# One pass of a hybrid decoder step rewritten as a pipeline in program order, sample group's linear attention moved to the third pass, PSUM banks divided anew

## The chip, the cores and the metric

The kernel runs on one core of a Trainium2 chip. The metric is device time in microseconds (us), measured over several executions; a profiled execution gives the trace. Before: 3477.97 us, median of 3 runs (3465.1 to 3479.64).

## The reference

One inference step of a two-layer decoder over a prompt of 4096 tokens and a sample group of 32 tokens (8 sequences of 4), model width 1024, in fp32:

```python
def even_layer(x, s5_state0, gla_state0, p):              # layer 0
    proj = rms_norm(x, p['norm_g']) @ p['w_in']
    u, gate_a, q, k, v, a_low, gate_b = split(proj)       # 512,512,256,256,512,16,512
    y, s5_last = s5_scan(u, s5_state0, ...)               # 32 groups, 64 complex states
    z = gelu(y)
    z = z * sigmoid(z @ p['w_glu'] + p['b_glu'])
    out_a = z * silu(gate_a)
    log_a = log_sigmoid(a_low @ p['w_gate'] + p['b_gate']) / 16
    o, gla_last = gla_chunked(q / 8, k, v, log_a, gla_state0)   # 4 heads, 64 x 128 states
    out_b = rms_norm(o, p['gla_norm_g']) * silu(gate_b)
    return x + concat([out_a, out_b]) @ p['w_out'], s5_last, gla_last
# layer 1: windowed grouped-query attention (window 128, 16 heads, sink logits), output projection
```

Outputs are both groups' activations and all new states.

## The kernel before

Every fp32 product on TensorE is made of three fp16 products: x and the weights are split into a high and a low part (xh, xl; wh, wl), scaled by powers of two, and `mmB` (L327, L328, L329) or `mmA` (L336, L337, L338) runs xh·wh, xl·wh, xh·wl into one PSUM bank, an `mm` tile. A power of two needs a bound on the weights, so each weight block is loaded twice: once for the bound (`bound_all`, loads at L221, squares by row at L192 on ScalarE and L195 on VectorE) and once to be split (`load_w`, L240 and L241).

The prompt is worked in 16 windows of 256 tokens, in passes:

- **Pass A** (`phaseA`, L683): per window, load x (L254, four tiles of 256 KB, 12 buffers), square it (ScalarE L756), add the squares (VectorE L760, L763, L764), sum over channels with a tiny matmul (L766), take the power -1/2 on GpSimd (L287), broadcast it (`rbcast`, L297 and L300), multiply and split x (`xsplit`: x times rb L311 on VectorE, xh L312 on ScalarE, xl L313 on GpSimd), then the projection to u, 96 matmuls with weights wuh and wul. u is evicted at L813 and stored to DRAM (u_d, L822) by ScalarE. `stage` holds all up to the statistics and returns `split`. Tables for the scan (`tables`, lines around L500 to L590) and the weights of pass B (`loads`) are made beside it.
- **Pass B** (`phaseB`, L866): per window a second load of x, projections to gate b, q, k, v (`instream`), the chunked linear attention (`core`, L1031 on; `head_norm` L1003, `og_split` L1019 to L1025, results stored as ob), pieces of the scan of the S5 branch (`s5_units`; U is loaded from u_d at L626), and `bounds` for the weights still to come. In windows 14 and 15 (SMP0, SMP1) the sample group's linear attention is added (`sample`, L1093): its projections (L351, folded at L367), then 8 states of 128 KB, each loaded, updated by L1232 and L1234 and stored.
- **Pass C** (`phaseC`, L1314): gate a, the half-GLU, the output projection, the rest of the sample group's first layer in windows 0 to 3.
- **Phase 2** (L1540 on): the second layer.

`merge` (L44) interleaves Python generators by their given costs; a scheduler then orders the instructions of each engine by priority in a simulated time of its own. `high_priority(HP)` around `stage` and `split` lets them move ahead of all else. Each DMA stands in the queue of the engine that issues it and keeps that queue's order: most are SyncE's (SP).

PSUM has 8 banks. Before, pass A uses four for `mm` tiles (pm0, pm1, pmx0, pmx1), three for small tiles `pt` (pta, ptb, ptc) and one for the scan (p0v); pass B two for `mm`, three for `pt`, one for the scan, two for the attention (pat); pass C three and two. `Rota` takes the banks of its list in turn:

```python
pms = self.pms = Rota(self.pta, self.ptb, self.ptc)     # pass A
pmm = Rota(*pm, *(self.pool(f"pmx{i}", es=ea, space=PSUM) for i in range(2)))
pmm, pms = Rota(*self.pm), Rota(self.pta, self.ptb, self.ptc)            # pass B
merge((ustream(), 170.0), (tables(), 18.0), (loads(), 66.0))             # end of pass A
merge((core(w), 14.0), (instream(w + 1), 46.0), (self.some(s, SB), SB), side)   # window of B
```

Of the kernel before, what the change touches and what calls it, by code (L numbers as in the profile page):

```python
# [9 lines left out]
F32 = mybir.dt.float32  # L10
F16 = mybir.dt.float16
# [9 lines left out]
SEQ = 4096  # L21
# [11 lines left out]
SB, SB1, BG, SC = 8.0, 14.0, 13.0, 14.0  # L33
SMP0, SMP1 = 14, 15
# [54 lines left out]
class K:  # L89
# [592 lines left out]
    def phaseA(self):  # L682
# [25 lines left out]
        pm = [self.pool(f"pm{i}", space=PSUM) for i in range(2)]  # L708
# [14 lines left out]
        wp = self.pool("w0", bufs=2, es=ea, side="right")  # L723
# [26 lines left out]
        def stage(n, blk0, xs):  # L750

            ps = pms.tile([128, 512], F32, name="pt")
            m = min(n, 128)
# [10 lines left out]
            nc.vector.tensor_add(sq[:, 0], sq[:, 0], sq[:, 1])  # L764
            for i in range((n + 127) // 128):
                nc.tensor.matmul(ps[0:m, i:i + 1], sq[:, 0, 128 * i:128 * i + m], self.onesf[:, 0:1],  # L766
                                 start=(i == 0), stop=True, skip_group_check=True)
            self.rms(ps, n, self.rst0, blk0, wp, self.rs0)

            def split():  # L770
                rb = self.rbcast(self.rst0, blk0, n, wp, pms, tag="pt")
                return self.xsplit(xs, n, rb, hp)

            return split

        xsm = stage(NS, 32, xsm)()
        xw = [x0] + [self.xload(xp, I["xT"], 256 * i, 256) for i in (1,)]
        x0 = stage(256, 0, x0)()
        xw.append(self.xload(xp, I["xT"], 512, 256))
# [3 lines left out]
        def ustream():  # L783

            x, nextx = xsm, x0
            split = stage(256, 2, xw[1])
            us = wp.tile([128, 4, 4, 8], F32, name="uss", bufs=1)
            ps = pmm.tile([128, 2, 256], F32, name="mm")
            for ct in range(4):
                self.mmB(ps[:, 0, NS * ct:NS * ct + NS], wuh, wul, 0, 128 * ct, *x)  # L790
# [69 lines left out]

    def phaseB(self):
# [11 lines left out]
        pmm, pms = Rota(*self.pm), Rota(self.pta, self.ptb, self.ptc)  # L875
# [4 lines left out]
        self.sog_d = self.dr.tile([128, 2, 4, NS], F16, name="sog_d")  # L880
# [15 lines left out]
        sr2 = self.scaled(ri, 2.0**-11, "sr2")  # L896
        sr8 = self.scaled(ri, 2.0**-13, "sr8")
# [105 lines left out]
        def head_norm(po, gb, m):  # L1003

            Q = Pc if m > NS else self.smp
            ss = Q.tile([128, 4], F32, name="ss", bufs=2)
            og = Q.tile([128, 512], F32, name="og", bufs=2) if m > NS else Q.tile([128, 512], F32, name="p")
            for h in range(4):
                nc.scalar.activation(og[0:m, 128 * h:128 * h + 128], po[h], AF.Square, bias=0.0, scale=1.0,
                                     accum_out=ss[0:m, h:h + 1])  # L1010
            nc.vector.tensor_scalar(ss[0:m], ss[0:m], 1.0 / 128, EPS, op0=OP.mult, op1=OP.add)  # L1011
            rs = Q.tile([128, 4], F32, name="rs", bufs=2)
            nc.gpsimd.tensor_tensor(rs[0:m], ss[0:m], self.mhalf[0:m, 0:4], op=OP.pow)  # L1013
            nc.vector.tensor_scalar(rs[0:m], rs[0:m], 2.0**-20, None, op0=OP.mult)
            for h in range(4):
                s = slice(128 * h, 128 * h + 128)
                nc.vector.scalar_tensor_tensor(og[0:m, s], po[h], rs[0:m, h:h + 1], gb[0:m, s], op0=OP.mult, op1=OP.mult)
            return og

        def og_split(og, m, oh, ol, t):  # L1020
            pt = pms.tile([128, 4, 128], F32, name="pt")[:, :, 0:m]
            for h in range(4):
                nc.tensor.transpose(pt[:, h], og[0:m, 128 * h:128 * h + 128], self.identf[0:m, 0:m])
            nc.scalar.activation(oh[:, :, t], pt, AF.Copy, bias=0.0, scale=1.0)
            nc.vector.tensor_sub(ol[:, :, t], pt, oh[:, :, t])  # L1025

        def core(w):
            W = Ws[w]
            yield 2.0
            for b in range(2):  # L1030
# [46 lines left out]
                og = head_norm([pa[0][:, 2], pa[1][:, 2], pa[0][:, 3], pa[1][:, 3]], W["gb"][b], 128)  # L1077
# [1148 lines left out]
```

## Time and profile before

| | us |
|---|---|
| median of 3 runs | 3477.97 (3465.1 to 3479.64) |
| the profiled execution's own time | 3474.53 |
| its span, first to last instruction | 3472.7 |
| PE (TensorE matmul) busy | 3178.1 (92%) |
| VectorE (DVE) busy | 2038.0 (59%) |
| ScalarE (ACT) busy | 1688.3 (49%) |
| GpSimd (POOL) busy | 1305.8 (38%) |
| mean granted TensorE clock | 0.951 |
| pass A | 0 to 352 |
| pass B, from its first to its last projection | 371 to 1317 |
| pass C, from its first matmul | 1377 |
| phase 2 | 1965 to 3472 |

A busy time counts an instruction's whole duration, so PE is also "busy" where its clock is halved. A wait names the instruction that stood still, the one it waited for, and the time lost. SPq is the queue of DMAs that SyncE issues; "L626 <- DMA ud<-us" there means that a load at L626 stood until a store of us to ud had landed, and all behind it in the queue stood too.

### The profile page before, as it was taken

To read this page: it belongs to the slowest core of one execution; us is meant where nothing else is said; L and a number is where in the kernel's file an instruction comes from. 1 tells how busy PE (TensorE), PEld (TensorE's weight loads), DVE (VectorE), ACT (ScalarE), POOL (GpSimd) and SP (SyncE) were. 2 spreads that over 40 slices of the span, in tenths; PEclk is the share of its full clock that TensorE was granted. 3 is DMA by queue.
4 is the path that set the end of the run, shared out by engine and by line. 5 is a ranking of instruction groups with operands and counts; after the bars stand their busy time and mean duration, and the time that the engine had idled before them with its cause. 6 is when DMAs were issued, how large, how long until landed. Compare 5 with 4: busy or idle time off the path is not lost.

```text
span 3472.7 us, 69409 instructions
## 1 busy us (share of the span) xinstructions
PE 3178.1 (92%) x27160; PEld 2472.0 (71%) x27160; DVE 2038.0 (59%) x4837; ACT 1688.3 (49%) x4044; POOL 1305.8 (38%) x1459
## 2 busy tenths in 40 slices
PE   4667798888989897999999999999999999999999
PEld 3556576666767665788888866777777777777777
DVE  6743576766567644543333357666666666666666
ACT  5444455445454642432222236655555555555565
POOL 4623322323232210122122265555555545555552
PEclk9878898999999996999999999999999999999999
DMA  7554644322232414544344322111111111111111
GB/s 190 106 114 86 183 132 118 88 61 78 59 78 68 133 51 123 176 124 110 104 120 118 87 48 64 38 37 36 36 42 40 40 40 40 40 40 40 40 30 41
DMA packets 359370, 277.72 MB, mean 80 GB/s; under 512 B 157985, under 2 KB 313585, under 8 KB 358897
## 3 DMA queue, kind: packets, MB, share of 16 engines
q1 hardware_dynamic: 316032, 231.28, 24.9%
q10 hardware_dynamic: 38912, 33.58, 3.7%
q0 software_dynamic: 4096, 8.43, 0.7%
q8 instruction: 213, 3.49, 0.4%
q14 instruction: 117, 0.95, 0.1%
HBM read 194.49 MB, written 78.50 MB: 79 GB/s over the span
## 4 chain that ended last, share of the span: by engine, by line
PE 64%; DMA 11%; DVE 10%; ACT 6%; issue 5%; POOL 3%; SPq 1%; ACTq 0%; DVEq 0%; POOLq 0%
PE mm L327 11%; PE mm L328 11%; PE mm L329 11%; PE mm L336 6%; PE mm L338 6%; PE mm L337 6%; DMA wst<-in_w_in 4%; PE po L1845 3%; DMA x<-in_xT 2%; PE pt L1803 2%; PE ps L1784 1%; PE ps L1785 1%; DVE z L638 1%; POOL xl L313 1%; PE pt L1653 1%
## 5 line engine op out<-in xcount | busy, mean ns | idle before, releaser
L313 POOL TENSOR_TENSOR xl<-x,xh 128x512 f16<-128x512 f32 (+1 forms) x196 | 236.0, 1223 | 359.6 <-ACT xh L312 351.4
L1768 ACT ACTIVATE Sc<-Sc,ng,rq 128x128 f32<-128x128 f32 x512 | 245.9, 482 | 138.7 <-DVE ng L1762 138.4
L327 PE MATMUL mm<-ogh,woh 128*128 128x256 f16 x960 | 261.7, 273 | 1.8 <-DVE xr L1889 1.8
L328 PE MATMUL mm<-ogl,woh 128*128 128x256 f16 x960 | 261.7, 273 | 0.7 <-POOL ogl L1857 0.7
L329 PE MATMUL mm<-ogh,wol 128*128 128x256 f16 x960 | 261.7, 273 | 0.0
L1796 POOL TENSOR_TENSOR Pl<-Sc,Ph 128x512 f16<-128x512 f32 x128 | 153.0, 1196 | 283.6 <-ACT Ph L1795 223.1
L337 PEld LDWEIGHTS <-xh 128*128 128x128 f16 x1536 | 155.8, 101 | 130.1 <-issue 43.9
L336 PEld LDWEIGHTS <-xh 128*128 128x128 f16 x1536 | 156.2, 102 | 119.9 <-ACT xh L312 16.3
L338 PEld LDWEIGHTS <-xl 128*128 128x128 f16 x1536 | 156.1, 102 | 115.0 <-issue 6.9
L328 PEld LDWEIGHTS <-woh 128*128 128x128 f16 x2112 | 206.8, 98 | 38.9 <-issue 15.5
L327 PEld LDWEIGHTS <-woh 128*128 128x128 f16 x2112 | 207.2, 98 | 27.1 <-issue 3.7
L329 PEld LDWEIGHTS <-wol 128*128 128x128 f16 x2112 | 206.9, 98 | 24.4 <-issue 1.8
L336 PE MATMUL mm<-wi1gbh,xh 128*128 128x264 f16 x512 | 155.9, 305 | 50.3 <-DVE k L995 18.9
L268 POOL TENSOR_TENSOR acc<-acc,sq 128x512 f32<-128x512 f32 x48 | 61.9, 1289 | 367.6 <-ACT sq L267 367.6
L1013 POOL TENSOR_TENSOR rs<-ss,mhalf 128x4 f32<-128x4 f32 (+1 forms) x33 | 36.8, 1114 | 372.7 <-DVE ss L1011 326.7
L327 PE MATMUL mm<-xh,wuh 128*128 128x256 f16 (+1 forms) x544 | 154.0, 290 | 19.7 <-ACT xh L312 19.3
L328 PE MATMUL mm<-xl,wuh 128*128 128x256 f16 (+1 forms) x544 | 154.4, 290 | 9.1 <-POOL xl L313 9.1
L338 PE MATMUL mm<-wi1gbh,xl 128*128 128x264 f16 x512 | 153.6, 303 | 3.6 <-POOL xl L313 3.6
L337 PE MATMUL mm<-wi1gbl,xh 128*128 128x264 f16 x512 | 155.4, 305 | 0.0
L329 PE MATMUL mm<-xh,wul 128*128 128x256 f16 (+1 forms) x544 | 154.2, 289 | 0.0
L327 PE MATMUL mm<-oh,woh 128*128 128x256 f16 x512 | 140.2, 274 | 10.9 <-DVE xr L1419 9.6
L1805 ACT ACTIVATE PT<-pt 128x1024 f16<-128x1024 f16 x128 | 129.3, 1011 | 39.9 <-PE pt L1803 39.9
(728 smaller groups left out, 10980.7 us busy)
## 6 DMA issues: line engine op xcount, KB each, us to landing
wst<-in_w_in SPq DMA_DIRECT2D x132, 256.0 KB
x<-in_xT SPq DMA_DIRECT2D x128, 256.0 KB
xr<-in_xT SPq DMA_DIRECT2D x64, 256.0 KB
h_d<-xr SPq DMA_DIRECT2D x64, 256.0 KB
x<-h_d SPq DMA_DIRECT2D x64, 256.0 KB
xr<-h_d SPq DMA_DIRECT2D x64, 256.0 KB
out_yT<-xr SPq DMA_DIRECT2D x64, 256.0 KB
wst<-in_w_out SPq DMA_DIRECT2D x48, 256.0 KB
```

Of the source, the lines that this page charges most:

```text
L313: nc.gpsimd.tensor_sub(l, x, h)
L327: nc.tensor.matmul(ps, wh[:, k0 + k, c], xh[k], start=(k == 0), stop=False)
L328: nc.tensor.matmul(ps, wh[:, k0 + k, c], xl[k], start=False, stop=False)
L329: nc.tensor.matmul(ps, wl[:, k0 + k, c], xh[k], start=False, stop=(k == n - 1))
L336: nc.tensor.matmul(ps, xh[k][:, t], wh[:, k, c0:c1], start=(k == 0), stop=False)
L337: nc.tensor.matmul(ps, xh[k][:, t], wl[:, k, c0:c1], start=False, stop=False)
L338: nc.tensor.matmul(ps, xl[k][:, t], wh[:, k, c0:c1], start=False, stop=(k == n - 1))
L1768: nc.scalar.activation(Sc[:, i], Sc[:, i], AF.Exp, bias=ng[:, i:i + 1], scale=scale[:, i:i + 1], accum_out=de[:, i:i + 1])
L1796: nc.gpsimd.tensor_sub(Pl, Sc, Ph)
L1803: nc.tensor.transpose(pt[:, a, i], s[:, i], self.ident16)
L1805: nc.scalar.activation(PT, pt.rearrange("p a i n -> p (a i) n"), AF.Copy, bias=0.0, scale=1.0)
L1845: nc.tensor.matmul(po[c].rearrange("p i n -> p (i n)"), vx[:, c], pend2[kv][1][p2][:, 4 * lo:4 * lo + 4].rearrange("p i n -> p (i n)"), st ...
```

## The change

1. **Pass of u.** `stage` and its closure become `squares`, `statistics` and `split`; `high_priority` goes. Windows 0 and 1 are made ready ahead of the loop. In window i, `split` of window i+1 and the load of window i+3 stand at the start, `squares` of i+2 after the first quarter of the projection, `statistics` of i+2 after the first half. The pool `w0` (sq, us, rb) moves to the left side of SBUF.
2. **PSUM.** Three `pm` banks for projections in all passes; the small banks are two (ptc goes); pass A has one further `mm` bank.
3. **Sample group.** In pass B, windows 8 and 9 now do its four projections, and store them unfolded to DRAM (sp_d). The folds, gates and 8 state updates (`sample_gla`) run in pass C, where the sample takes windows 0 to 9 with cost 3.4 each, not 0 to 3 with 4.0. `bounds` therefore has windows 0 to 7 to run in. `head_norm` and `og_split` become methods.

```diff
-SB, SB1, BG, SC = 8.0, 14.0, 13.0, 14.0
-SMP0, SMP1 = 14, 15
+SB, SB1, BG, SC = 8.0, 14.0, 13.0, 7.0
+SMP0, SMP1, SMP2 = 8, 9, 10
...
-        pm = [self.pool(f"pm{i}", space=PSUM) for i in range(2)]
+        pm = [self.pool(f"pm{i}", space=PSUM) for i in range(3)]
...
-        self.ptc = self.pool("ptc", es=self.eps, space=PSUM)
-        pms = self.pms = Rota(self.pta, self.ptb, self.ptc)
+        pms = self.pms = Rota(self.pta, self.ptb)
...
-        pmm = Rota(*pm, *(self.pool(f"pmx{i}", es=ea, space=PSUM) for i in range(2)))
+        pmm = Rota(*pm, self.pool("pmx", es=ea, space=PSUM))
...
-        wp = self.pool("w0", bufs=2, es=ea, side="right")
+        wp = self.pool("w0", bufs=2, es=ea)
...
-                    x = nextx
-                    i = 4 * w + h + 1
-                    if i < 16:
-                        with self.tc.high_priority(HP):
-                            nextx = split()
-                            if i + 2 < 16:
-                                xw.append(self.xload(xp, I["xT"], 256 * (i + 2), 256))
+                    i = 4 * w + h
+                    if 1 <= i < 15:
+                        x.append(split(256, 2 * (i + 1), xw[i + 1]))
+                        if i + 3 < 16:
+                            xw.append(load(i + 3))
...
-                            self.mmB(ps[:, k], wuh, wul, 0, 256 * c + 128 * k, *x)
+                            self.mmB(ps[:, k], wuh, wul, 0, 256 * c + 128 * k, *x[i])
+                            if c + k == 0 and i + 2 < 16:
+                                sq = squares(256, xw[i + 2])
...
-                        if c == 0 and i + 1 < 16:
-                            with self.tc.high_priority(HP):
-                                split = stage(256, 2 * (i + 1), xw[i + 1])
+                        if c == 0 and i + 2 < 16:
+                            statistics(256, 2 * (i + 2), sq)
...
-        pmm, pms = Rota(*self.pm), Rota(self.pta, self.ptb, self.ptc)
+        pmm, pms = Rota(*self.pm), Rota(self.pta, self.ptb)
...
+            for b, c0, c1 in (("gb", 0, 512), ("gb", 512, 528), ("qk", 0, 512), ("v", 0, 512)):
+                p = self.keep(Q.tile([128, 512], F32, name="p"), self.parts(*W1[b], 0, c0, c1, x, pmm))
+                nc.sync.dma_start(self.sp_d[b, c0][:, 0:c1 - c0], p)
+                yield 3.0
...
-                  (self.some(smp, 4.0) if w < 4 else None, 4.0))
+                  (self.some(smp, 3.4) if w < SMP2 else None, 3.4))
```

The order of SP's DMAs in the middle of pass A, before. Rows with "x4" stand for several in a row; x is a load of pass A's next windows, U a load for the scan from what ScalarE stored as ud, wst weights.

```order
56 L626 DMA U<-ud_0_119 16x4x64 x3
57 L254 DMA x<-in_xT 128x2x256 x6
58 L626 DMA U<-ud_0_119 16x4x64
59 L254 DMA x<-in_xT 128x2x256
60 L626 DMA U<-ud_0_119 16x4x64 x2
61 L254 DMA x<-in_xT 128x2x256
62 L626 DMA U<-ud_0_119 16x4x64 x5
63 L254 DMA x<-in_xT 128x2x256 x8
64 L626 DMA U<-ud_0_123 16x4x64 x6
65 L254 DMA x<-in_xT 128x2x256
66 L626 DMA U<-ud_0_123 16x4x64 x2
67 L254 DMA x<-in_xT 128x2x256 x3
```

In the changed kernel no U is loaded within pass A; the first is at its row 105. Its order at the end of pass A: rows 89 to 93 end with the last loads of x of pass A, row 101 is the first of pass B. Of rows 94 to 100, one load is the last of load_w and 39 are the bounds' (in_w_in, in_w_glu and in_w_out are the weights in DRAM).

```order
89 L254 DMA x<-in_xT 128x2x256 x2
90 L221 DMA wst<-in_w_in 128x512
91 L254 DMA x<-in_xT 128x2x256
92 L221 DMA wst<-in_w_in 128x512
93 L254 DMA x<-in_xT 128x2x256
94 L221 DMA wst<-in_w_in 128x512 x9
95 L221 DMA wst<-in_w_glu 128x512 x4
96 L221 DMA wst<-in_w_out 128x512 x13
97 L912 DMA wga<-in_w_gate 16x256
98 L914 DMA bga<-in_b_gate 128x2
99 L221 DMA wst<-in_w_out 128x512 x3
100 L221 DMA wst<-in_w_in 128x512 x11
```

Before, pass B's first x (row 122 of that order) stands ahead of all of the bounds' loads; now 39 of them stand ahead of it.

PE at the end of pass B, before: L1240, L1232 and the L1023 with a 128x32 output are the sample group's, the others belong to the core of windows 14 and 15; pass C's first matmul comes four rows behind the last one shown.

```order
11950 L1240 MATMUL pt<-identf,z 32x128 x4
11951 L1232 MATMUL pt<-v,p 64x128 x8
11952 L1051 MATMUL pt<-identf,kt 128x128 x4
11953 L1023 MATMUL pt<-identf,p 128x32 x4
11954 L1023 MATMUL pt<-identf,og 128x128 x4
11955 L1072 MATMUL pt<-v,kT 64x128 x4
11956 L1023 MATMUL pt<-identf,og 128x128 x4
11957 L1072 MATMUL pt<-v,kT 64x128 x4
11958 L1066 MATMUL pa_14472<-Sm,q_14077 128x128
11959 L1066 MATMUL pa_14473<-Sm,q_14077 128x128
11960 L1066 MATMUL pa_14472<-Sm,q_14172 128x128
11961 L1066 MATMUL pa_14473<-Sm,q_14172 128x128
```

The same place in the changed kernel (L885 is og_split, L1041, L1065, L1070, L1076 the core).

```order
11911 L1076 MATMUL pt<-v,kT 64x128 x4
11912 L885 MATMUL pt<-identf,og 128x128 x2
11913 L1041 MATMUL pa_14231<-q_14009,k_14010 128x128
11914 L1041 MATMUL pa_14231<-q_14101,k_14102 128x128
11915 L885 MATMUL pt<-identf,og 128x128
11916 L1041 MATMUL pa_14232<-q_14009,k_14010 128x128
11917 L1041 MATMUL pa_14232<-q_14101,k_14102 128x128
11918 L885 MATMUL pt<-identf,og 128x128
11919 L1065 MATMUL pa_14231<-v,attm_3536 128x128 x2
11920 L1070 MATMUL pa_14231<-Sm,q_14009 128x128
11921 L1070 MATMUL pa_14231<-Sm,q_14101 128x128
11922 L1065 MATMUL pa_14232<-v,attm_3537 128x128 x2
```

None of the sample group's rows is left here; four rows further on pass C's first matmul follows, and og_split's last transposes come behind it.

## Rows read from the trace of the kernel before

**Rows 1.** Page, part 1: each engine's busy time, share of the span, instructions

```profile
PE 3178.1 (92%) x27160; PEld 2472.0 (71%) x27160; DVE 2038.0 (59%) x4837; ACT 1688.3 (49%) x4044; POOL 1305.8 (38%) x1459
```

**Rows 2.** Windows: span, us; busy us (instructions) per engine; clock; DMA share, GB/s

```profile
150.00:200.00 50.00, 29.41 (x212) 23.29 (x212) 26.02 (x37) 19.98 (x34) 20.54 (x20) 0.74 0.50 86
200.00:250.00 50.00, 38.20 (x303) 32.16 (x301) 25.73 (x45) 24.90 (x40) 16.35 (x16) 0.83 0.60 122
250.00:300.00 50.00, 40.53 (x297) 32.66 (x298) 22.20 (x45) 23.50 (x44) 15.44 (x15) 0.80 0.67 122
300.00:325.00 25.00, 14.70 (x116) 12.21 (x114) 17.29 (x21) 12.20 (x19) 12.29 (x10) 0.80 0.36 89
325.00:350.00 25.00, 25.00 (x232) 22.42 (x230) 0.00 (x0) 8.15 (x9) 5.14 (x7) 1.00 0.16 57
350.00:375.00 25.00, 8.90 (x58) 7.13 (x56) 14.29 (x21) 8.61 (x16) 11.79 (x11) 0.64 0.69 193
375.00:700.00 325.00, 286.86 (x2038) 214.38 (x2036) 220.93 (x605) 168.10 (x428) 96.22 (x102) 0.91 0.43 124
700.00:1150.00 450.00, 408.49 (x2993) 308.30 (x2991) 296.69 (x786) 219.97 (x538) 114.77 (x122) 0.93 0.26 67
...
1250.00:1325.00 75.00, 71.21 (x595) 51.66 (x592) 30.64 (x126) 34.81 (x107) 11.71 (x13) 0.96 0.11 36
1325.00:1375.00 50.00, 31.81 (x158) 19.81 (x158) 17.54 (x62) 6.08 (x28) 3.57 (x4) 0.50 0.43 135
1375.00:1400.00 25.00, 23.87 (x205) 18.91 (x203) 15.53 (x38) 14.01 (x29) 0.67 (x1) 0.95 0.83 239
1400.00:1965.00 565.00, 549.72 (x5016) 487.18 (x5016) 224.50 (x348) 169.75 (x272) 122.05 (x117) 0.99 0.43 118
```

**Rows 3.** Waits of SP's DMA queue, 50 to 365 us: total us, times, longest

```profile
SPq L626 <- DMA ud<-us: 48.4, 7, 13.9
SPq L254 <- POOL xl L313: 44.8, 22, 7.9
...
SPq L254 <- DMA ud<-us: 19.2, 2, 14.4
```

**Rows 4.** Groups by line, 100 to 350 us: busy us, mean ns, idle before and releasers

```profile
L327 PE MATMUL mm<-xh,wuh 128*128 128x256 f16 x435 | 127.1, 293 | 2.4 <-ACT xh L312 2.4
...
L756 ACT ACTIVATE sq<-x 128x512 f32<-128x512 f32 x43 | 26.6, 626 | 77.6 <-DMA x<-in_xT 64.2 <-DMA ud<-us 12.4 <-DVE sq L760 0.6
...
L766 PE MATMUL pt<-onesf,sq 128*128 128x1 f32 x48 | 9.2, 296 | 54.2 <-DVE sq L764 24.1 <-ACT Ks L544 20.9 <-DVE X L589 9.2
```

**Rows 5.** Waits of PE, 365 to 1215 us: total us, times, longest

```profile
PE mm L336 <- DVE k L995: 18.9, 6, 4.9
PE pt L1023 <- DVE og L1017: 16.2, 5, 7.6
PE mm L336 <- DVE gb L946: 12.3, 4, 5.6
```

**Rows 6.** Chain that ended last, 1310 to 1380 us: start, duration, engine, work

```profile
1335.96 2.19 DMA out_gla_s<-S
1338.16 2.46 DMA S<-in_gla
1340.75 0.36 DVE S L1234
...
1359.72 0.61 ACT ogh L1024
1360.35 0.69 DVE ogl L1025
1361.07 5.73 DMA ob<-ogl
...
1368.49 8.95 DMA xl<-xp
```

**Rows 7.** PE groups by line, 1150 to 1375 us: busy us, mean ns, idle before

```profile
L1232 PE MATMUL pt<-v,p 32*64 32x128 f32 x64 | 10.8, 432 | 9.7 <-DVE S L1234 5.9 <-DVE p L1227 3.8
```

More of the change, by code (lines that the diff above doesn't have):

```diff
@@ L764, in stage, with statistics, split, ready @@
             nc.vector.tensor_add(sq[:, 0], sq[:, 0], sq[:, 1])
+            return sq[:, 0]
+        def statistics(n, blk0, sq):
+            ps = pms.tile([128, 512], F32, name="pt")
+            m = min(n, 128)
             for i in range((n + 127) // 128):
-                nc.tensor.matmul(ps[0:m, i:i + 1], sq[:, 0, 128 * i:128 * i + m], self.onesf[:, 0:1],
+                nc.tensor.matmul(ps[0:m, i:i + 1], sq[:, 128 * i:128 * i + m], self.onesf[:, 0:1],
                                  start=(i == 0), stop=True, skip_group_check=True)
             self.rms(ps, n, self.rst0, blk0, wp, self.rs0)
[L770 to L779, printed above, removed]
+        def split(n, blk0, xs):
+            return self.xsplit(xs, n, self.rbcast(self.rst0, blk0, n, wp, pms, tag="pt"), hp)
+        def ready(n, blk0, xs):
+            statistics(n, blk0, squares(n, xs))
+            return split(n, blk0, xs)
+        load = lambda i: self.xload(xp, I["xT"], 256 * i, 256)
+        xsm = ready(NS, 32, xsm)
+        xw = [x0, load(1)]
+        x = [ready(256, 0, x0)]
+        xw.append(load(2))
+        x.append(ready(256, 2, xw[1]))
+        xw.append(load(3))
         nc.sync.dma_start(self.g1, I["g1"])
@@ L859, in rbload, with head_norm, og_split @@
         return rb
+    def head_norm(self, Q, po, gb, m):
+        nc = self.nc
+        ss = Q.tile([128, 4], F32, name="ss", bufs=2)
+        og = Q.tile([128, 512], F32, name="og", bufs=2) if m > NS else Q.tile([128, 512], F32, name="p")
+        for h in range(4):
+            nc.scalar.activation(og[0:m, 128 * h:128 * h + 128], po[h], AF.Square, bias=0.0, scale=1.0,
+                                 accum_out=ss[0:m, h:h + 1])
+        nc.vector.tensor_scalar(ss[0:m], ss[0:m], 1.0 / 128, EPS, op0=OP.mult, op1=OP.add)
+        rs = Q.tile([128, 4], F32, name="rs", bufs=2)
+        nc.gpsimd.tensor_tensor(rs[0:m], ss[0:m], self.mhalf[0:m, 0:4], op=OP.pow)
+        nc.vector.tensor_scalar(rs[0:m], rs[0:m], 2.0**-20, None, op0=OP.mult)
+        for h in range(4):
+            s = slice(128 * h, 128 * h + 128)
+            nc.vector.scalar_tensor_tensor(og[0:m, s], po[h], rs[0:m, h:h + 1], gb[0:m, s], op0=OP.mult, op1=OP.mult)
+        return og
+    def og_split(self, pms, og, m, oh, ol, t):
+        nc = self.nc
+        pt = pms.tile([128, 4, 128], F32, name="pt")[:, :, 0:m]
+        for h in range(4):
+            nc.tensor.transpose(pt[:, h], og[0:m, 128 * h:128 * h + 128], self.identf[0:m, 0:m])
+        nc.scalar.activation(oh[:, :, t], pt, AF.Copy, bias=0.0, scale=1.0)
+        nc.vector.tensor_sub(ol[:, :, t], pt, oh[:, :, t])
     def phaseB(self):
@@ L1001, in instream @@
                 prep(w + 1)
[L1003 to L1025, printed above, removed]
         def core(w):
@@ L1087, in finish @@
                 tiles[:] = [P.tile([128, 4, NW], F16, name=f"og{x}") for x in "hl"]
-            og_split(og, 128, *tiles, slice(128 * b, 128 * b + 128))
+            self.og_split(pms, og, 128, *tiles, slice(128 * b, 128 * b + 128))
             if b == 1:
@@ L1144, in sample @@
-            lm = Q.tile([128, 4, n], F32, name="z")
-            l, bb = lm[:, 0:2], lm[:, 2:4]
-            pg = pmi.tile([128, 512], F32, name="pt")
-            for j in range(2):
-                g = pg[:, n * j:n * j + n]
-                nc.tensor.matmul(g, wga[:, 128 * j:128 * j + 128], alT, start=True, stop=True)
-                nc.scalar.activation(l[:, j], g, AF.Abs, bias=bga[:, j:j + 1], scale=1.0)
-                nc.vector.tensor_scalar(bb[:, j], g, bga[:, j:j + 1], 0.0, op0=OP.add, op1=OP.min)
@@ L1152, in sample @@
-            nc.scalar.activation(l, l, AF.Exp, bias=0.0, scale=-1.0)
-            nc.scalar.activation(l, l, AF.Ln, bias=1.0, scale=1.0)
-            for j in range(2):
-                for c in range(0, n, 4):
-                    t = slice(c, c + 4)
-                    nc.vector.tensor_tensor_scan(bb[:, j, t], bb[:, j, t], l[:, j, t], 0.0, op0=OP.add, op1=OP.subtract)
-            yield 0.5
-            p = proj("qk")
-            yield 1.5
-            qz = Q.tile([128, 2, 2, n], F32, name="q")
@@ L1440, in sample @@
         def sample():
+            sog = []
+            yield from sample_gla(sog)
             n, Q = NS, self.smp
```

295 lines of the change are left out of this document (157 added, 138 removed).

## The prediction

> **What bounds the kernel now.** I read the page's busy times first: PE is busy 92% of the span [rows 1], so a gain must come from the 8% that is left or from time in which PE is busy at half clock. The table by stretches says where these lie [rows 2]. Read its second number (PE busy) against the width of the stretch, and the number behind the engines (the clock). From 1400 us on pass C runs at 549.7 of 565 us and clock 0.99: nothing to win. Phase 2, unchanged, is left out. Three places are loose. Between 150 and 325 us, in the pass of u, PE is busy 122.8 of 175 us at clocks of 0.74 to 0.83. In pass B (375 to 1150) it is idle 38.1 + 41.5 us, at 0.91 to 0.93. From 1325 to 1375, between the passes B and C, it is busy 31.8 of 50 us at 0.50, the lower of its two levels (1.2 of 2.4 GHz) throughout.
>
> Next, what each waits for. In the pass of u ScalarE's squares stood 64.2 us for loads of x, and PE 54.2 us for the statistics [rows 4]. The loads of x were late because SP's queue stood: 48.4 us at a U load and 19.2 us at an x load behind it, each for a store of us to land [rows 3]. A third wait there, 44.8 us for xl, is the 12 x buffers still being in use. In pass B the longest waits are for banks: L336 for the evictions of k and gb, 18.9 and 12.3 us, and og_split 16.2 us for og [rows 5]. At the end of B the chain goes through the sample group's states, one after the other: store, load, update, 2.19, 2.46 and 0.36 us [rows 6].
>
> **The change part by part.**
>
> *Pass of u.* No instruction of the windows is removed; they stand in another order, and the U loads leave this stretch. A window's projections are 96 matmuls, some 103 with its small ones. From 150 to 325 us PE ran 212 + 303 + 297 + 116 = 928 instructions [rows 2], so 9.0 windows, 19.4 us each. What would a window take without waits? PE: 25.00 us for 232 at clock 1.00 [rows 2], so 10.3 us for 96. VectorE: 91.2 us busy in the 175, so 10.1 per window. ScalarE 80.6, so 9.0. GpSimd 64.6, so 7.2. DMA: 50 x 0.50 + 50 x 0.60 + 50 x 0.67 + 25 x 0.36 = 97.5 us, so 10.8 per window. Four resources are within 2 us of each other, so the floor of 10.8 won't be reached with two windows of depth; a window in which each does its part once, with a wait or two of some us as in the rows, I put at 14.5. That is an estimate, 40% above PE's own time. The gain is 9 x (19.4 - 14.5) = **-44 us**; at the floor 9 x 8.6 = -77. The other end is above nothing: of PE's 54.2 us at L766, 20.9 + 9.2 are for tables' tiles (Ks, X) in the small banks [rows 4], and with two banks in place of three such waits may grow by half, +15. I lean to the gain, since ScalarE reads these tiles, and its stillness was the late x.
>
> Moved with it: 39 of the bounds' loads (256 KB each, 10.2 MB) come ahead of pass B's first x on SP's queue, with their squares on ScalarE and VectorE. At the fastest rate shown, 239 GB/s [rows 2], they take 43 us. They start with the last x load of pass A, some three and a half windows ahead of its end, 51 us at 14.5 each, and run beside them with DMA to spare. I cost them at nothing; if that cover is short, pass B's first x waits for them, up to +25.
>
> *Three banks for projections, two small ones.* The waits for k and gb, 31.2 us [rows 5], are L336 starting a tile in a bank whose reader isn't done. With the orders of both kernels and the rows' durations, I estimate that 21 of 116 tiles of pass B get their bank back within 4 us before, and 3 of 120 after: some 27 us go. Against that, of 150 small tiles 7 had under 4 us between uses before, and 33 after, though only 3 under 2.5. A small tile is held 0.61 + 0.69 us by its two readers [rows 6] when they come at once, so few of the 33 wait, about +3. Together **-24 us**. Bounds: all of these waits and what half clock follows them, -45; or each of the 33 waits 1.3 us and the gain is nil, +43.
>
> *Sample group out of windows 14 and 15.* Its projections (L351) move to windows 8 and 9 and cost the same there. The folds, state matmuls and waits go: **-8 us**, near the 10.8 us of L1232 [rows 7], of which part lies in the next term (0 to -20).
>
> *The end of B.* From 1317 to 1377 no projection runs, 60 us, through eight states of some 6 us each [rows 6]. Without them the last core of window 15 remains, then og_split, the store of ob (5.73) and the load of x for pass C (8.95) [rows 6]. By the order, pass C's first matmuls now stand ahead of og_split's last transposes. I take 35 us: **-25 us**; -10 if the last core is as slow as the states were, -35 if it hides.
>
> *Sample group in pass C.* PE is full there [rows 2], so all it adds counts. Its state matmuls (10.8 us at half clock, so about 5), its reading, folds and small matmuls make 12 us; a projection bank stays with the sample while the states load, which I put at 8 more, from the 9.7 us that L1232 waited [rows 7]. **+20 us** (+8 to +45).
>
> **Sum:** -44 - 24 - 8 - 25 + 20 = -81 us against the profiled execution's own 3474.5 us (span 3472.7), which lies 3.5 under the median: 3393.5, so **3393 us**.
>
> *A rule against the change.* The row first: in the 150 us from 150 to 300 the 16 DMA engines were busy 0.50 to 0.67 of the time, while SP stood 48.4 us for stores [rows 2, 3]. The Trainium skill, "DMA: Bandwidth & Descriptors", section "Issuing engines are not separate DMA queues", says that DMAs started by any engine run on the same 16 engines and interleave there, so that starting them elsewhere saves only the starting. By that rule late x loads are late in the transfer, and clearing SP's queue wins nothing. The trace speaks for the queue: the share leaves a third to a half free. That is the second case below.
>
> **The rivals.**
>
> 1. *Small banks bound pass B (slower).* PE issues in order; when a small tile's bank isn't free, every projection behind it stands too. For: og_split waited up to 7.6 us for VectorE [rows 5], and a late VectorE also holds the small tiles it reads. Against: the short gaps that I estimate are mostly over 2.5 us, twice the 1.3 us of a hold. The other terms give -57, the third bank -27. To be slower by 17 us the 150 small tiles must cost 101 us, so the point is 0.67 us each. At 1 us each: 3474.5 - 84 + 150 = 3540 us.
> 2. *Transfers bound the pass of u.* The bounds' loads come into it, the pace stays at 19.4 less little, and what is won is lost ahead of pass B. For: the DMA's 10.8 us per window is the largest of the four. Against: the shares. Without that term: 3437 us.
> 3. *The sample group costs pass C what it saved B.* The states' loads (2.46 us, two buffers) hold a bank, and small tiles wait on both. +45 instead of +20: 3418 us.
> 4. *The pipeline isn't one.* By the order, statistics now come a fixed 144 u matmuls ahead of their window, where before, with priority, they came 191 to 306 ahead for most. The lead shrinks; if lead and not the queue was the limit, the 54.2 us of L766 stay and grow, +15: 3452 us.
>
> **How the numbers follow.** Chances: forecast 0.46; rival 1 0.13; rival 2 0.18; rival 3 0.12; rival 4 0.11. About 0.5%, 17 us, is what a measurement of this kernel can tell from no change. Faster by that is under 3460: the forecast, rivals 2 and 3 nearly whole, more than half of rival 4, and what of rival 1 stays small: 0.79. Slower, over 3495: most of rival 1 and the tail of 4: 0.12. The rest 0.09. The forecast's own range is 3340 to 3440: the pass of u between 11 and 17 us per window moves it by about 30 either way, the rest by 20. The range for 8 in 10 goes from 3325, both the pass of u and the banks near their better bounds, to 3465, which takes in rivals 2 to 4 and leaves rival 1 out.
>
> **What would show it.** In the profile of the changed kernel the pass of u should end near 308 us, with PE at over 0.9 of each stretch and the squares' wait for x gone; statistics should no longer lead PE's waits there. If instead SP's queue stands for wst, or x of pass B lands 30 us behind the last u matmul, it is rival 2. In pass B the waits for k and gb should be under 8 us, and waits named pt should stay where they were; if pt waits add to over 100 us, it is rival 1. The stretch from the last projection of B to C's first should be 35 us. Pass C should last 608 us, against 588. The prediction is wrong if the pass of u keeps 19 us per window though SP never stands for ud.

## The result, and the profile after the change

The changed kernel takes 3425.58 us (median of 4 runs, 3419.85 to 3432.8); beside it the kernel before took 3476.81 us. The ratio is 0.986, 95% interval 0.983 to 0.989, so 51 us faster. The forecast was 3393 us, 84 us under that median, with a range of 3325 to 3465: the direction and the range held, the forecast gain was 33 us too large. The profiled execution took 3428.2 us with a span of 3426.4, 46.3 us under the span before.

Part 1 of the page after, against [rows 1]:

```profile
PE 3149.3 (92%) x27160; PEld 2453.6 (72%) x27160; DVE 2051.1 (60%) x4838; ACT 1686.8 (49%) x4044; POOL 1311.1 (38%) x1459
```

PE has the same 27160 matmuls and 28.8 us less busy time: a shorter busy time for the same work means fewer of them at half clock (mean granted clock 0.951 before, 0.96 after). Where the span went is seen by marks, read from the timeline of PE (us; "last of C" is the last matmul with the output weights; the first projection and the first matmul of pass C are the very first ones, where the table of times before has 371 and 1377):

| | before | after | difference of the stretch |
|---|---|---|---|
| last matmul of the pass of u | 352.2 | 346.3 | -5.9 |
| first projection of pass B | 363.8 | 366.6 | +8.8 |
| first matmul of pass C | 1372.1 | 1282.7 | -92.2 |
| last of C | 2004.8 | 1950.9 | +35.4 |
| end | 3472.7 | 3426.4 | +7.7 |

The stretches add up to -46.2. Pass B with its end is the whole gain, the pass of u gave next to nothing, and pass C took back over a third of what pass B gave. The table by stretches of the changed kernel, with the columns of [rows 2]:

```profile
150.00:200.00 50.00, 42.34 (x321) 34.58 (x322) 22.85 (x35) 22.98 (x37) 20.97 (x18) 0.85 0.37 99
200.00:250.00 50.00, 34.74 (x271) 27.77 (x270) 32.66 (x50) 28.93 (x46) 17.15 (x14) 0.83 0.62 145
250.00:300.00 50.00, 37.77 (x306) 31.88 (x304) 31.79 (x56) 28.02 (x52) 22.07 (x18) 0.86 0.76 149
300.00:325.00 25.00, 17.09 (x144) 14.67 (x143) 5.49 (x13) 6.44 (x14) 6.84 (x6) 0.86 0.57 124
325.00:350.00 25.00, 17.09 (x125) 13.21 (x123) 11.71 (x25) 13.11 (x27) 5.73 (x6) 0.85 0.61 191
350.00:375.00 25.00, 4.87 (x22) 3.08 (x23) 5.13 (x13) 7.59 (x15) 10.34 (x9) 0.50 0.76 235
375.00:700.00 325.00, 300.04 (x2225) 226.93 (x2223) 230.58 (x625) 170.32 (x424) 96.70 (x106) 0.94 0.36 100
700.00:1150.00 450.00, 412.58 (x3181) 312.86 (x3180) 317.37 (x789) 234.96 (x582) 128.64 (x136) 0.95 0.31 84
```

Between 150 and 325 us PE now ran 321 + 271 + 306 + 144 = 1042 instructions, against 928 before, 12% more. But before, the last 25 us of the pass ran at full speed (232 instructions from 325 to 350); now they run 125, and DMA is busier there (0.61, against 0.16). Counted by the windows' own u matmuls (96 each), the twelfth of the 16 windows ends at 292.9 us before and at 272.4 now, and the last four take 59.4 and 74.0 us. So the pass gained 20 us in its middle and lost 15 at its end. In pass B, from 375 to 1150 us, PE ran 5406 instructions against 5031 [rows 2], at a clock of 0.94 to 0.95 against 0.91 to 0.93.

What SP's queue waited for from 50 to 365 us, against [rows 3]:

```profile
SPq L254 <- POOL xl L313: 92.7, 35, 15.6
SPq L221 <- ACT wst L192: 54.0, 21, 7.6
...
SPq L254 <- DMA ud<-us: 9.2, 2, 6.5
```

The 48.4 us at U loads are gone, as the order said. The wait of x loads for the splits that free x buffers grew from 44.8 to 92.7 us. And 54.0 us stand at loads for bounds (L221), each for a square of ScalarE (L192) that frees its buffer; before, this wait was 19.3 us. Of the 54.0, the part from 290 us on belongs to the bounds that the change moved here, with their three buffers:

```profile
SPq L221 <- ACT wst L192: 36.3, 16, 7.5
```

ScalarE in its turn stood for the transfers of these loads, from 275 to 347 us:

```profile
ACT wst L192 <- DMA wst<-in_w_out: 16.1, 5, 8.3
ACT wst L192 <- DMA wst<-in_w_in: 12.1, 4, 6.4
...
ACT wst L192 <- DMA wst<-in_w_glu: 4.3, 2, 3.2
```

Its squares of x still waited for x from 100 to 350 us, nearly as long as the 64.2 us of [rows 4]:

```profile
ACT sq L753 <- DMA x<-in_xT: 56.2, 28, 7.8
```

And PE, from 100 to 365 us:

```profile
PE pt L297 <- POOL rst L287: 35.7, 7, 8.3
PE pt L768 <- DVE sq L761: 9.8, 3, 4.6
```

The wait for the statistics, 54.2 us in [rows 4], fell to 12.3 us at L768 (9.8 and 2.5 for another engine); a wait one step later in the same chain, the broadcast for the next window at L297 behind the power on GpSimd, took its place with 35.7 us (before: 3.2). The two together went from 57.4 to 48.0 us. The waits of pass B, against [rows 5] (365 to 1200 us):

```profile
PE pa L1041 <- DVE og L878: 14.7, 5, 6.5
...
PE mm L336 <- DVE k L1023: 7.2, 5, 4.3
```

The wait for gb (12.3 us) is gone, that for k fell from 18.9 to 7.2. At the end of pass B the chain has no states any more; from the last projection (1256.0) to pass C's first matmul there are 26.7 us, before 55.1 (1317.0 to 1372.1).

### The profile page after: what moved, and what is told of

The parts are those of the page before. It is cut to its first block, busy times and chain, and to the rows that moved or that the text cites. A ratio compares the mean times of both kernels' runs of the same rounds, so it can differ in the third digit from the quotient of the medians.

```text
span 3426.4 us, 69488 instructions
## 1 busy us (share of the span) xinstructions
PE 3149.3 (92%) x27160; PEld 2453.6 (72%) x27160; DVE 2051.1 (60%) x4838; ACT 1686.8 (49%) x4044; POOL 1311.1 (38%) x1459
## 3 DMA queue, kind: packets, MB, share of 16 engines
q1 hardware_dynamic: 316784, 232.75, 25.3%
## 4 chain that ended last, share of the span: by engine, by line
PE 63%; DVE 12%; DMA 10%; ACT 6%; issue 5%; POOL 2%; SPq 1%; ACTq 0%; DVEq 0%; POOLq 0%
PE mm L327 11%; PE mm L329 11%; PE mm L328 11%; PE mm L336 6%; PE mm L338 6%; PE mm L337 6%; DMA wst<-in_w_in 3%; PE po L1864 3%; PE pt L1822 2%; POOL xl L313 1%; DMA x<-in_xT 1%; DMA x<-h_d 1%; PE ps L1803 1%; PE ps L1804 1%; DMA wst<-in_w_out 1%
## 5 line engine op out<-in xcount | busy, mean ns | idle before, releaser
L327 PE MATMUL mm<-obh,woh 128*128 128x256 f16 x512 | 141.9, 277 | 7.8 <-DVE xr L1286 6.7
```

What stands on the lines that cost most here:

```text
L327: nc.tensor.matmul(ps, wh[:, k0 + k, c], xh[k], start=(k == 0), stop=False)
```

## The experiments

They ran on three further chips, K, L and M, on which the kernel before took 3460.8, 3460.1 and 3461.2 us (medians); each ratio is to the kernel before on the same chip, with its 95% interval. The changed kernel was run again on M alone, so a run on K or L is set against it across chips. Marks are us of one profiled execution: the end of the pass of u; the length of pass B from its first projection to pass C's first matmul; the length of pass C to its last matmul. Single executions of one kernel lie up to 34 us apart (pipe_only, 3441.9 to 3475.6), so differences of some us in marks tell nothing.

| run | chip | us | ratio | end of u | B | C |
|---|---|---|---|---|---|---|
| after_again | M | 3408.45 | 0.9844 (0.983 to 0.9859) | 329.3 | 913.4 | 667.6 |
| no_pipe | K | 3420.32 | 0.9897 (0.9865 to 0.9929) | 330.9 | 917.8 | 662.9 |
| w0_right | K | 3424.6 | 0.9891 (0.986 to 0.9922) | 324.2 | 940.6 | 672.0 |
| no_psum | K | 3475.27 | 1.004 (1.0027 to 1.0054) | 323.9 | 976.0 | 671.2 |
| two_two | L | 3473.89 | 1.0034 (1.0018 to 1.005) | 327.7 | 976.3 | 667.5 |
| no_sample | K | 3414.87 | 0.9864 (0.9846 to 0.9881) | 335.3 | 963.0 | 623.1 |
| psum_only | L | 3443.42 | 0.9952 (0.9933 to 0.9972) | 343.4 | 988.1 | 626.3 |
| pipe_only | L | 3460.31 | 0.9999 (0.9978 to 1.002) | 329.3 | 1015.9 | 632.9 |
| smp_13_14 | L | 3411.24 | 0.9861 (0.9835 to 0.9888) | 329.6 | 960.5 | 627.3 |
| smp_13 | M | 3409.52 | 0.9843 (0.9818 to 0.9869) | 324.5 | 963.8 | 633.8 |
| loads_after | M | 3375.68 | 0.975 (0.9724 to 0.9776) | 294.8 | 919.2 | 667.1 |
| x_lead | M | 3375.94 | 0.9751 (0.9736 to 0.9766) | 299.3 | 921.4 | 669.8 |

**The changed kernel again**, for comparison.

> The changed kernel itself on this chip, so that the other runs stand beside it: ratio 0.983 to 0.989 as on the first chip, with the pass of u ending between 324 and 346 us.

Its ratio is as on the first chip. The pass of u ends 17 us earlier here than in the first chip's profile (346.3), so ends of this pass are not compared with the first chip's. Chips K, L and M agree in the median of the kernel before; that they agree in this mark too is not shown.

**Taking one part away: the order of the pass of u.**

```diff
-                    i = 4 * w + h
-                    if 1 <= i < 15:
-                        x.append(split(256, 2 * (i + 1), xw[i + 1]))
+                    x = nextx
+                    i = 4 * w + h + 1
+                    if i < 16:
+                        with self.tc.high_priority(HP):
+                            nextx = split()
...
```

> The changed kernel with the old pass of u (stage and split at high priority, in the old order); banks, the place of pool w0 and the sample group as changed. The pass of u ended at 346 us in the changed kernel and at 352 before. Theory: the new order by itself is worth little, since both orders are held by late transfers and by engines that wait in program order; the pass of u ends within 10 us of 346 and the total is within 10 us of 3425. Rival: the new order is worth the 44 us that I forecast and something else (the bounds' loads) took them back; then this kernel ends its pass of u 30 us or more later and takes 3455 us or more.

The theory held: the pass ends at 330.9 us with the old order (chip K) and 329.3 with the new (M). The totals' intervals lie just apart (0.9865 and 0.9859 are their near ends, on two chips), so the new order may be worth some us, but not the 44. This holds with the U loads out of the pass.

**The place of w0.**

```diff
-        wp = self.pool("w0", bufs=2, es=ea)
+        wp = self.pool("w0", bufs=2, es=ea, side="right")
```

> The changed kernel with pool w0 on the right side again, so that the scan's U loads come back into the pass of u and the 39 loads of the bounds leave its end. Theory (these loads, with the squares that ScalarE and VectorE do on them ahead of the last evictions, hold the end of the pass and pass B's first x): from the 290 us mark on this kernel gains 15 to 25 us, but SP stands for stores of us again, some 60 us in all, most of it beside other work; total 3405 to 3425 us. Rival (the U loads behind stores are what made x late): SP's waits for ud return and with them the pass ends at 352 us or later, total 3435 us or more.

Neither side came out whole. SP stands for stores of us again, less than I expected (24.7 and 14.7 us):

```profile
SPq L626 <- DMA ud<-us: 24.7, 6, 17.5
...
SPq L254 <- DMA ud<-us: 14.7, 1, 14.7
```

The pass ends at 324.2, so U loads in it cost about as much as the bounds' loads that they replace. The place of one pool decides which of the two stands in SP's queue. The total is 16 us above the changed kernel's all the same: pass B starts at 335.2 in place of 350.9 but takes 27 us longer, and why is not shown.

This run also says what made the middle of the pass faster. From 150 to 200 us, psum_only below (old order, U loads in the pass) and this run (new order, U loads in the pass):

```profile
150.00:200.00 50.00, 30.15 (x198) 23.33 (x199) 18.91 (x33) 19.11 (x31) 16.06 (x15) 0.74 0.42 84
```

```profile
150.00:200.00 50.00, 41.81 (x362) 35.92 (x360) 21.29 (x36) 23.18 (x37) 21.07 (x19) 0.93 0.43 104
```

198 instructions of PE (chip L) against 362 (K); no_pipe (old order, no U loads) has 316 (K) and the changed kernel 376 (M). So either edit, the new order or the removal of the U loads, brings most of the gain in the middle, and the two together little more.

**The banks.**

```diff
-        pm = [self.pool(f"pm{i}", space=PSUM) for i in range(3)]
+        pm = [self.pool(f"pm{i}", space=PSUM) for i in range(2)]
...
-        pmm, pms = Rota(*self.pm), Rota(self.pta, self.ptb)
+        pmm, pms = Rota(*self.pm), Rota(self.pta, self.ptb, self.ptc)
```

> The changed kernel with the old division of banks: pass B has two banks for projections and three small ones, pass A four and three. Theory (a third projection bank is worth 24 us, two small ones cost 3): 3450 us, with the waits for the evictions of k and gb back at some 30 us. Rival (what the small banks cost eats the gain): 3415 to 3430 us.

Far more than the 24 us: without the new banks the rest of the change is slower than the kernel before. From 0.9844 to 1.004 the banks are worth 0.0196 x 3461 = 68 us, of which pass B holds 976.0 - 913.4 = 62.6. The waits for evictions say little of it (in this kernel, 370 to 1205 us):

```profile
PE mm L336 <- DVE gb L975: 10.6, 5, 6.0
PE mm L336 <- DVE k L1024: 6.9, 2, 5.1
```

17.5 us, against 6.3 in the changed kernel on chip M; all named waits of PE there add to 99 and 71 us. The whole of pass B shows the rest. First this kernel, then the changed one:

```profile
345.80:1321.90 976.10, 856.98 (x6245) 645.53 (x6245) 617.83 (x1637) 474.80 (x1184) 260.91 (x276) 0.91 0.30 85
```

```profile
350.90:1264.20 913.30, 831.91 (x6242) 626.37 (x6243) 618.42 (x1627) 468.13 (x1180) 259.97 (x275) 0.94 0.32 91
```

PE is idle 119.1 us without and 81.4 with the third bank: 37.7 us. And the same number of matmuls, within three, is busy 857.0 and 831.9 us: 25.1 us, at a mean clock of 0.91 and 0.94. Together that is the difference in length of pass B. Idle time gained was forecast, though from the waits for k and gb alone, which are 11 of the 28 us of named waits; the clock that comes with it stood only in the bound.

**Two banks for projections and two small ones in pass B.**

```diff
-        pmm, pms = Rota(*self.pm), Rota(self.pta, self.ptb)
+        pmm, pms = Rota(*self.pm[0:2]), Rota(self.pta, self.ptb)
```

> The changed kernel, but pass B uses only two of the three projection banks, and still two small ones: one bank of pass B is left empty. Against the run with the old division (two and three, ratio 1.004) it shows the price of two small banks alone, against the changed kernel the worth of the third projection bank alone. Theory by my terms (small banks +3 us): 1.003 to 1.008. Rival 1 in its weaker form (small banks do cost, some 0.2 us per tile, 30 us): 1.012 or more.

1.0034, and pass B is 976.3 us long, as with three small banks (976.0). Beside two projection banks the third small bank was worth nothing; rival 1 is out, also in its weaker form. What two small banks cost beside three projection banks was not measured apart from the gain.

**The sample group back in pass B** (with its functions as before).

```diff
-SB, SB1, BG, SC = 8.0, 14.0, 13.0, 7.0
-SMP0, SMP1, SMP2 = 8, 9, 10
+SB, SB1, BG, SC = 8.0, 14.0, 13.0, 14.0
+SMP0, SMP1 = 14, 15
...
```

> The changed kernel with the sample group's linear attention back in windows 14 and 15 of pass B. Theory by my terms (-8 for the windows, -25 for the end of B, +20 for pass C): 13 us slower than the changed kernel, 3438 us, with some 60 us without projections between B and C and pass C back at about 590 us. Rival 3 (pass C pays all that B saves): within 5 us of 3425, with B longer and C shorter by the same 35 to 45 us.

Rival 3 came out. Pass B grows by 963.0 - 913.4 = 49.6 us, pass C shrinks by 667.6 - 623.1 = 44.5, and the second layer by 6; the totals' intervals overlap, so the move is worth nothing that these runs can tell. PE in pass C, with the sample group (1264 to 1932 us of the changed kernel) and without (1320 to 1943 us of this one):

```profile
1264.00:1932.00 668.00, 634.94 (x5703) 550.85 (x5704) 276.34 (x481) 200.80 (x341) 141.74 (x137) 0.98 0.45 121
```

```profile
1320.00:1943.00 623.00, 609.67 (x5559) 538.18 (x5557) 259.11 (x408) 192.33 (x315) 138.13 (x132) 0.99 0.45 123
```

25.3 us more busy and 19.7 us more idle. The waits that are longer in the changed kernel:

```profile
PE mm L327 <- DVE xr L1286: 11.0, 4, 6.2
PE pt L1446 <- DVE p L1441: 6.1, 1, 6.1
PE pt L885 <- DVE p L878: 5.6, 1, 5.6
```

L1446 and L885 are the sample group's own steps; all projections of pass C stand behind them in PE's order.

**The banks alone**, an edit of the kernel before.

```diff
-        pm = [self.pool(f"pm{i}", space=PSUM) for i in range(2)]
+        pm = [self.pool(f"pm{i}", space=PSUM) for i in range(3)]
...
-        pmm, pms = Rota(*self.pm), Rota(self.pta, self.ptb, self.ptc)
+        pmm, pms = Rota(*self.pm), Rota(self.pta, self.ptb)
```

> The kernel before with the new division of PSUM banks alone (three for projections, two small ones; the pass of u four and two). Theory after the first four runs (the banks are the whole gain, the new pass of u and the sample group's move are worth nothing to speak of): ratio to the kernel before 0.984 to 0.988, with pass B, from its first projection to pass C's first, 45 us shorter. Rival (the banks pay only together with the new pass of u, which hands pass B another order): 0.995 or more.

The rival's number, 0.9952: 17 us, with pass B 20 us shorter than before on the first chip (988.1 and 1008.3). But pipe_only (next) and no_sample differ by the banks alone as well, with the new pass of u: 0.9999 and 0.9864, 47 us, and pass B 1015.9 and 963.0. So the banks are worth 17 us with the old pass of u and 47 us with the new one, which by itself is worth nothing. What in the new pass of u does that is not shown. That the bounds' loads are gone from pass B can't be all of it: in x_lead they stand in pass B again, and it takes 921.4 us, 8 more than in the changed kernel.

**The pass of u alone**, an edit of the kernel before.

```diff
-        wp = self.pool("w0", bufs=2, es=ea, side="right")
+        wp = self.pool("w0", bufs=2, es=ea)
...
-                            nextx = split()
...
+                        x.append(split(256, 2 * (i + 1), xw[i + 1]))
```

> The kernel before with the new pass of u alone (program order, no high priority, pool w0 on the left), old banks, sample group in windows 14 and 15. Theory: ratio 0.995 to 1.003, the end of the pass of u some 5 us earlier and its first projections of pass B later behind the bounds' loads. Rival (the pass of u is worth more than the change showed, since with two small banks it is held there): 0.99 or less, with the pass of u ending 20 us earlier.

0.9999, as the theory had it; the pass ends 14 us earlier and not 5, at 329.3 against 343.4 with the old one (psum_only), but pass B's first projection comes at 350.4 against 354.8, and pass B wins nothing.

**The sample group one window earlier in pass B**, an edit of the run no_sample.

```diff
-SMP0, SMP1 = 14, 15
+SMP0, SMP1 = 13, 14
```

> New banks and new pass of u, but the sample group's linear attention stays in pass B, in windows 13 and 14 and not 14 and 15, so that window 15 follows it. Theory (the move to pass C is a wash: pass C pays by waits what the end of B saves; the chain of states need only not be the last thing in pass B): the stretch from the last projection of B to C's first falls from 65 to about 30 us while pass C stays at 623 us, ratio 0.976 to 0.980. Rival (the states' chain holds pass B wherever it stands, since PE waits in order): no gain over windows 14 and 15, 0.985 to 0.988.

No gain: 60 us remain between B's last projection and C's first, since by PE's order a good part of the states still came last. So once more with a larger share:

```diff
-SB, SB1, BG, SC = 8.0, 14.0, 13.0, 14.0
-SMP0, SMP1 = 14, 15
+SB, SB1, BG, SC = 8.0, 14.0, 13.0, 34.0
+SMP0, SMP1 = 13, 14
```

> As the run with the sample group in windows 13 and 14, but with a share in the merge of 34 in place of 14, so that its last state stands ahead of pass B's last projections in PE's order. Theory (in windows 13 and 14 half of the states were still left when the projections ended, so the tail stayed): the stretch from B's last projection to C's first falls from 60 to 30 us and pass C stays at 625; the total is 25 us under that run, ratio 0.977 to 0.981. Rival (the states' chain stops PE as long inside pass B as behind it): pass B to its last projection grows by what the tail loses, ratio 0.985 to 0.988.

By the stretches its rival held: the end falls to 44 us (1265.8 to 1309.8), and pass B up to its last projection grows from 900.1 to 919.8; the ratio, 0.9843, lies between the two forecasts. Wherever it stands, the sample group's linear attention costs some 45 to 50 us.

**The weights behind the pass of u.**

```diff
-        merge((ustream(), 170.0), (tables(), 18.0), (loads(), 66.0))
+        merge((ustream(), 170.0), (tables(), 18.0))
+        merge((loads(), 66.0))
```

> The changed kernel, but the bounds and the split of pass B's weights (loads) are merged behind the pass of u and not beside it; all x loads of the pass now stand ahead of them on SP's queue. Theory (the pass is held because weights stand between its x loads on SP and between its squares and splits on ScalarE and VectorE, where each piece waits for its own transfer): the pass of u falls to some 14 us per window, as I had put it, and ends at 240 to 270 us; the weights then cost what they took, and the total is 3400 to 3440 us on this chip. Rival (the chain of statistics and split through five engines, or the DMA engines, hold the pass without the weights too): it ends within 15 us of the changed kernel's, and the total is 3450 us or more.

**x loaded four windows ahead.**

```diff
-        xp = self.pool("x0", bufs=12, es=ea, side="right")
+        xp = self.pool("x0", bufs=16, es=ea, side="right")
...
-                        if i + 3 < 16:
-                            xw.append(load(i + 3))
+                        if i + 4 < 16:
+                            xw.append(load(i + 4))
```

> The changed kernel with x loaded four windows ahead in place of three (16 buffers in place of 12). Theory (x is late because its loads stand behind weights on SP, not because they are issued too late): the squares still wait for x and the pass of u ends within 8 us of the changed kernel's. Rival (the lead of the loads was the limit): the wait of the squares for x falls by half and the pass ends 15 us or more earlier, ratio 0.981 or less.

Both end the pass 30 to 34 us earlier and take 3376 us, 33 us under the changed kernel: better than both kernels compared. For x_lead my theory was wrong by its number, and the rival's right. For loads_after neither side came out: the pass did not end at 240 to 270 us, and it did end 34 us earlier, with a total under both forecasts. What the squares waited for x from 100 to 345 us, in the changed kernel, loads_after and x_lead:

```profile
ACT sq L753 <- DMA x<-in_xT: 45.7, 27, 4.6
```

```profile
ACT sq L753 <- DMA x<-in_xT: 51.9, 37, 5.3
```

```profile
ACT sq L753 <- DMA x<-in_xT: 19.8, 9, 7.0
```

The two passes are equally short with 51.9 and with 19.8 us, so late x is not what sets the end of this pass. But the orders show that both edits did a second thing: with other pools and another order the bounds' loads no longer stand ahead of pass B's first x, and the U loads don't come back. The windows tell where the time was won. The twelfth ends at 254.8 (changed), 245.6 (loads_after) and 252.1 us (x_lead), so the first twelve moved by 3 to 9 us. The last four take 74.6, 49.3 and 47.3 us. From some 262 us on the 39 bounds' loads stand in the changed kernel. In the seven other profiles with the new order and these loads there, the first chip's among them, the last four windows take 70 to 76 us too (no_pipe, with the old order: 63.9). The stretches 200 to 250 and 250 to 300, first the changed kernel on this chip:

```profile
200.00:250.00 50.00, 35.60 (x275) 28.80 (x275) 38.40 (x57) 31.55 (x56) 24.17 (x19) 0.90 0.71 157
250.00:300.00 50.00, 34.75 (x276) 29.16 (x275) 24.00 (x43) 23.66 (x44) 20.24 (x18) 0.87 0.79 157
```

then loads_after:

```profile
200.00:250.00 50.00, 46.29 (x398) 39.26 (x397) 24.27 (x36) 26.38 (x40) 27.06 (x24) 0.97 0.41 114
250.00:300.00 50.00, 41.81 (x384) 37.34 (x381) 17.22 (x34) 21.62 (x31) 19.51 (x19) 0.98 0.36 73
```

and x_lead:

```profile
250.00:300.00 50.00, 48.20 (x442) 42.90 (x439) 18.82 (x29) 23.02 (x34) 23.38 (x23) 1.00 0.51 76
```

A DMA share of 0.79 with 276 PE instructions, against 0.36 to 0.51 with 384 to 442, and a clock of 0.87 against 0.98 to 1.00. The waits of PE for the power (L297) fell with it, from 34.3 us to 15.1 and 13.6 (150 to 300 us):

```profile
PE pt L297 <- POOL rst L287: 34.3, 8, 6.6
```

```profile
PE pt L297 <- POOL rst L287: 15.1, 6, 7.5
```

That the 39 bounds' loads do not stand in the pass is what the two have in common; loads_after also moves the loads and the split of pass B's weights, which x_lead leaves in the pass, and x_lead changes the lead. A kernel that moves the bounds alone, with U left out, was not run, so the share of each is not separated, and the two edits were not tried together.

## Why the prediction was right, and where it was wrong

**What bounds the kernel.** The three loose places were the right ones: what was won was won in pass B and at its end, loads_after and x_lead won 30 us more in the pass of u, and phase 2 stayed (within 8 us).

**The pass of u (-44): wrong.** It gave -5.9 us, and the next stretch took 8.8 back. The failing step is the one on the 39 loads of the bounds: "I cost them at nothing", since 51 us of the pass lay beside them with DMA to spare. DMA had to spare (shares of 0.57 to 0.76 from 250 to 350 us), the engines' order had not. Each load waits for one of three buffers, which a square on ScalarE or VectorE frees, and these squares stand in the same order as the splits and the evictions of u. So a late transfer holds up what stands behind its square: ScalarE stood 32.5 us for these transfers from 275 to 347 us. The chain that ended last, in the changed kernel, goes through them:

```profile
316.37 8.71 DMA wst<-in_w_out
325.17 0.71 DVE wst L195 x2
325.90 5.16 DMA wst<-in_w_out
...
351.17 4.05 DMA wst<-in_w_in
...
356.52 0.39 SPq L254
...
358.55 5.93 DMA rb<-rs
364.64 5.57 POOL x L311 x4
```

Pass B's first x (SPq L254) is issued at 356.5, 10 us after the last u matmul: "up to +25" of that step was the right worry. The pace itself, 14.5 us per window without such waits, was right: in loads_after 10.3 windows are left at 150 us and end at 294.8, 14.0 us each; in x_lead it is 14.5. The pace before was read wrong. My 9.0 windows counted the matmuls of the tables too; 800 of the instructions from 150 to 325 us are the windows' own, 8.3 windows, 21.0 us each, and in the changed kernel 913, 18.4 us each. That is close to my own sign of being wrong, 19 us per window with SP never standing for ud; a rest of 9.2 us for ud was left.

Wrong too, in the main, was the reading that the squares waited for x because SP's queue stood at the U loads. Those waits are gone and the squares still wait 56.2 us for x, where I forecast none. The end that I forecast, 308 us, is missed by both sides: 295 to 299 without the bounds, 324 to 346 with them or U.

**Rival 2 (transfers, 3437 us) came out in the pass of u**, by its own account: the bounds' loads come into the pass and what is won there is lost ahead of pass B. The rule of the Trainium skill in "DMA: Bandwidth & Descriptors", section "Issuing engines are not separate DMA queues", fits the end of the pass and not its middle. In the middle the pass went faster at a lower share (0.37 from 150 to 200 us, with 321 instructions in place of 212), by the new order as much as by the missing U loads. At the end another kind of load took the same 16 engines (busy 0.57 to 0.76 from 250 to 350 us) and the same queue. Clearing a queue wins what the next load in it doesn't take.

**Three banks, two small ones (-24): right in sign, three times too small.** The mechanism held as far as it went: the waits for k and gb fell, and small banks cost nothing beside two projection banks (two_two). The term counted these waits alone; the runs give 62.6 us in pass B, 37.7 of it idle time, only 11 at k and gb, and 25.1 shorter busy time at a clock of 0.94 in place of 0.91. My bound of -45 was passed; the other bound was summed wrongly, since +43 for the small tiles against -27 is +16 and not nil. The term also depends on the others: 17 us alone, 47 with the new pass of u.

**Windows 14 and 15, the end of B, pass C (-8 - 25 + 20 = -13): nothing was left of the gain.** The end of B fell by 28.4 us (forecast 25). Taking the sample group out of B is worth 49.6 us (forecast 33), and it costs pass C 44.5 and the second layer 6 (forecast 20): rival 3, with its +45. The mis-sized term is pass C: 12 us of work, measured 25.3 us more busy, and 8 of stalls, measured 19.7.

**Rival 4** (the lead shrinks, +15) came in part: the wait at L766 fell by 42 us, but 30.1 of its 54.2 were for tables' tiles, and the wait one step on, at L297, grew by 32.5. With the bounds' loads gone L297 falls to 15.1 and 13.6, so most of it was these loads and not the lead. **Rival 1** is refuted by two_two.

So -81 became -46 by errors against each other, and that the time fell into the range is in part luck: 47 us of gain too much in and behind the pass of u and 23 us of cost too little for pass C and the second layer on one side, 35 us of gain too little for pass B and its end (92 against 57) on the other.

## What to carry to other kernels

When a change frees a queue, look in the new order at what moves up into the gap: here the place of one small pool decided whether U loads or 39 weight loads stood in SP's queue, and the pass of u ended within 5 us of the same place with either. An engine that works on a load stands until its transfer lands, and with it all that comes behind in its order. So loads for later work belong behind the stretch that can't afford them, even where the DMA engines have room. Where PE is mostly full, price a removed wait by the idle time and by the clock that it brings back, and price moved work with the stalls of its chain, not by its matmuls alone.

## What the runs showed of the hardware that was not expected

The third projection bank took 37.7 us of idle time out of PE in pass B, and the same matmuls then took 25.1 us less busy time, at a mean granted clock of 0.94 in place of 0.91. Here a wait taken away was worth 1.7 times its idle time. And beside two projection banks, two small banks in place of three changed the length of pass B by 0.3 us (976.3 and 976.0), though the projections issue in order behind every small tile. The price of loads for later work is seen in one number: with the new order the last four windows of the pass of u took 70 to 76 us with the bounds' 39 loads beside them and 47 to 49 us without, at DMA shares of 0.79 and of 0.36 to 0.51 from 250 to 300 us.
